# Six plain chunks instead of five at the start of three FFNs, and the normalised input formed in one piece on VectorE

## The chip, the core and the metric

The kernel runs on one core of a Trainium2 chip. The core has TensorE (PE in the rows; PEld is its weight load), VectorE (DVE), ScalarE (ACT), GpSimd (POOL) and SyncE (SP), which here only issues DMAs. The metric is the device time of one execution in microseconds; lower is better.

## What is computed

A small encoder on 528 tokens (16 meta tokens and 512 frames) of width 1024: two layers, each of an FFN, a token mixer and another FFN, with a residual add around each. There are thus four FFNs, and the change touches three of them. One FFN is

```python
def rmsnorm(x, g):
    xf = xf * lax.rsqrt(jnp.mean(xf * xf, axis=-1, keepdims=True) + EPS)
    return xf.astype(x.dtype) * g

def swiglu(h, w_gate, w_up, w_down):            # 1024 -> 2816 -> 1024
    return (jax.nn.silu(h @ w_gate) * (h @ w_up)) @ w_down

h = h + 0.5 * swiglu(rmsnorm(h, ffn1_norm[l]), ffn1_w_gate[l], ffn1_w_up[l], ffn1_w_down[l])
```

All data are float32.

## The kernel before

The residual `h` lies transposed: eight tiles of 128 channels by 528 tokens, one for each `c` of `KC = 8`. TensorE takes float32 products as three products of rounded halves: every operand is split into a high part (a ScalarE copy to `fp32r`) and a low part (a VectorE subtraction of the high part), and high·high, high·low and low·high are added in PSUM. For a weight tile of 128x1024 `fetch` does this: a DMA into `raw` (two buffers), the copy of L169, the subtraction of L170. For other tiles `split_to` does it (L183, L184). So each weight and each input costs VectorE an instruction of its own.

An FFN has 22 chunks `f` of 128 hidden channels. A *plain* chunk (`gate_up_plain`, L371) multiplies gate and up in the direct way: for gate and for up 8 pieces of K, 3 products of parts, 2 halves of the tokens, 96 matmuls in all. A *form* chunk (`gate_up`, L383) uses a Strassen-like scheme with 7 products in the place of 8: 7 x 4 x 3 = 84 matmuls. It needs sums of the weights (`bring_sums`, `bring`, `add_up`, `two_forms`, gathered in `prepare`) and sums of the input (`sums_x`, L245 to L248). `begun` is the number of the first form chunk: 5 in three FFNs, 2 in the third FFN of the program, whose input arrives normalised (`normed`).

The three FFNs without `normed` start with the 1/rms of their input unknown. `first_chunks` handles this. Chunks 0 and 1 run on the input without 1/rms, and their results are scaled later (chunk 0's are parked in `held`). Meanwhile 1/rms is found in two steps: `rms[0]` sums squares by matmul (L275), takes a power on GpSimd (L283) and puts the result on diagonals (L292, L294); `rms[1]` spreads it over all partitions by matmul (L303) and copies it out of PSUM (L307, L305). Then `normal_x` forms, for each of the eight `c`, the normalised input `xn` (L224) and splits it; chunk 2 runs by pieces of K (`by_chunk`), so that each piece can start when its `c` is split. From chunk 3 on the input is there.

The order on each engine is not the order of the source. When the program is built, a list scheduler places the instructions, with the source order as priority and its own estimate of when operands and buffers are there; what is ready earlier may go ahead. At run time each engine takes its queue in the placed order, and an instruction that waits holds up all that are behind it. Buffers come from pools: 48 slots for token tiles, 14 for split weights, 2 `raw`, 4 `half`, 4 `sum`, and 6 PSUM banks and one pair of banks.

The down products run one block of chunks later (`down_steps`, L193): eight parts `d` for each block, dealt out over three places in each form chunk. For block 1 (chunks 4 to 7) the number of places is three times the number of its form chunks: nine before.

Of the kernel before, what the change touches and what calls it, by code (L numbers as in the profile page):

```python
# [13 lines left out]
AF = mybir.ActivationFunctionType  # L14
ALU = mybir.AluOpType
# [10 lines left out]
KC = D // P  # L26
# [67 lines left out]
def trunk(ctx: ExitStack, tc, h0, wall, vecs, band, rope, out):  # L94
# [85 lines left out]

    def split_to(dst, src):

        nc.scalar.activation(dst[0], src, AF.Copy)  # L183
        nc.vector.tensor_tensor(dst[1], src, dst[0], op=ALU.subtract)  # L184

    def parts(T):
        return ((0, 264), (264, 528)) if T == L else ((0, T),)
# [30 lines left out]
    def normal_x(xs, c, g, t0, r):  # L218


        T = L - t0
        n = T // 2
        xn = xs["n"][c] = slot()[:, :T]
        nc.vector.scalar_tensor_tensor(xn, h[c][:, t0:L], gain(g + c), r, op0=ALU.mult, op1=ALU.mult)  # L224
        if c >= KC // 2:
            p = slot(F32R)[:, :T], slot(F32R)[:, :T]
            split_to(p, xn)
            xs["b"][c] = [(p[0][:, a : a + n], p[1][:, a : a + n]) for a in (0, n)]
            return
        xs["b"][c] = []  # L230
        for a in (0, n):
            t = slot(F32R)
            p = t[:, :n], t[:, n : 2 * n]
            split_to(p, xn[:, a : a + n])
            xs["b"][c].append(p)

    def sums_x(xs, k):


        xa, xb = xs["n"][k], xs["n"][k + KC // 2]  # L240
        T = xa.shape[-1]
        n = T // 2
        a1, a2, b1, b2 = (t[:, a : a + n] for t in (xa, xb) for a in (0, n))
        sub, stt = nc.vector.tensor_tensor, nc.vector.scalar_tensor_tensor
        sub(a1, a1, a2, op=ALU.subtract)  # L245
        sub(a2, b2, a2, op=ALU.subtract)
        stt(b2, b2, -1.0, a1, op0=ALU.mult, op1=ALU.subtract)
        stt(b1, b1, -1.0, b2, op0=ALU.mult, op1=ALU.subtract)  # L248
        out = []
        for t in (xa, xb):  # L250
            p = slot(F32R)[:, :T], slot(F32R)[:, :T]
            split_to(p, t)
            out += [(p[0][:, a : a + n], p[1][:, a : a + n]) for a in (0, n)]
        xs["t"][k] = [out[0], out[3], out[1], out[2]]
# [73 lines left out]
        return after  # L328


    def fetch_gate_up(u0, one=fetch):
        one(u0)
        one(u0 + 1)

    def ffn(u0, x, g, rms, t0, after, early=None, final=None, normed=None, hooks=()):

# [30 lines left out]
        def plain(w, o, xs, ks=range(KC)):  # L367
            for k in ks:
                for n, (a, b) in enumerate(((0, 0), (0, 1), (1, 0))):
                    for i, ps in enumerate(o):  # L370
                        nc.tensor.matmul(  # L371
                            ps,
                            w[a][:, k * P : k * P + P],
                            xs[k][i][b],
                            start=k == 0 and n == 0,
                            stop=k == KC - 1 and n == 2,
                        )
# [18 lines left out]
        def bring_sums(f):  # L396

            if f < NF:
                t = pair_of_sums()
                gate, up = wall[u0 + 3 * f], wall[u0 + 3 * f + 1]  # L400
                nc.sync.dma_start(t[:, 0], gate[:, :512])
                nc.sync.dma_start(t[:, 1], up[:, 512:])
                nc.gpsimd.dma_start(t, up[:, :512].unsqueeze(1).to_broadcast([P, 2, 512]), accum_op=ALU.add)  # L403
                forms[f] = {"s31": t}

        def bring(f):
            if f < NF:
                forms[f]["gate"] = load(u0 + 3 * f)
                t = forms[f]["up"] = half()
                nc.sync.dma_start(t, wall[u0 + 3 * f + 1][:, 512:])  # L410
# [39 lines left out]
        def evacuate(f, pg, pu, r=None):  # L450

            t, s = slot()[:, :T], slot()[:, :T]
            mult = nc.vector.tensor_tensor
            for ps, c0, c1 in pg:
                if r is None:
                    nc.scalar.activation(t[:, c0:c1], ps, AF.Silu)
                else:
                    mult(t[:, c0:c1], ps, r[:, c0:c1], op=ALU.mult)
            if r is not None:
                nc.scalar.activation(t, t, AF.Silu)  # L460
                mult(t, t, r, op=ALU.mult)
            for ps, c0, c1 in pu:
                mult(s[:, c0:c1], ps, t[:, c0:c1], op=ALU.mult)
            close(f, s)
# [8 lines left out]
        def gate_up_plain(f, by_chunk=False, pair=False):  # L473
            w_g, w_u = weights(f)
            pg = banks(2)
            pu = [ps for ps, _, _ in group_pair(T)] if T == L and (by_chunk or pair) else banks(2)
            if by_chunk:
                for k in range(KC):
                    plain(w_g, pg, x["b"], (k,))
                    plain(w_u, pu, x["b"], (k,))  # L480
                hook()
            else:
                plain(w_g, pg, x["b"])
                hook()
                plain(w_u, pu, x["b"])
            evacuate(f, by_halves(pg), by_halves(pu))
            hook()
# [42 lines left out]

        def first_chunks():

            nonlocal x
            w_g, w_u = weights(0)
            halves = [[(hi[:, a : a + N], lo[:, a : a + N]) for a in (0, N)] for hi, lo in x]
            pg, pu = banks(2), banks(2)
            for k in range(KC):
                for w, o in ((w_g, pg), (w_u, pu)):
                    plain(w, o, halves, (k,))
            held = []  # L540
            for o in (pg, pu):
                t = slot()[:, :T]
                for ps, c0, c1 in by_halves(o):
                    nc.scalar.activation(t[:, c0:c1], ps, AF.Copy)
                held.append([(t, 0, T)])
            fetch_gate_up(u0 + 3)
            rms[0]()
            w_g, w_u = weights(1)
            pg, pu = banks(2), banks(2)
            plain(w_g, pg, halves)  # L550
            r = rms[1]()
            fetch_gate_up(u0 + 6)
            xs = new_x()
            for c in range(KC):
                normal_x(xs, c, g, t0, r)
            plain(w_u, pu, halves)
            evacuate(1, by_halves(pg), by_halves(pu), r)
            x = xs
            fetch_gate_up(u0 + 9)
            sums_x(x, 0)  # L560
            gate_up_plain(2, True)
            fetch_gate_up(u0 + 12)
            sums_x(x, 1)
            sums_x(x, 2)
            gate_up_plain(3)
            bring_sums(5)
            bring(5)
            evacuate(0, *held, r)
            sums_x(x, 3)
            bring_sums(6)  # L570
            gate_up_plain(4, pair=True)
            prepare(5)
            bring(6)

        def first_chunk():
            nonlocal x
# [46 lines left out]

            return [lambda d=d: part(d) for d in range(KC)]

        begun = 5 if normed is None else 2
        for b, blk in enumerate(BLOCKS):

            n = 3 * sum(f >= begun for f in blk)
# [30 lines left out]
    x = []  # L660
# [622 lines left out]
```

## Time and profile before

| | |
|---|---|
| time, median of 3 runs | 1699.82 us (1695.87 to 1700.03) |
| profiled execution, its own time | 1702.0 us |
| its span, first to last instruction | 1700.2 us |
| PE, PEld busy | 1637.3, 1555.5 us |
| DVE, ACT, POOL busy | 1142.5, 809.5, 221.9 us |
| mean granted TensorE clock | 0.981 |

Busy times are sums over the whole span. A stretch with other limits than the rest does not show in them; it is seen in the slices, in the windows of a stretch, and in what each engine waited for. A row of the timeline gives the start of a merged group of instructions, its length, the engine, the line, the operation and the count, and in brackets the idle time in front of it with the instruction that ended it.

### The profile page before, as it was taken

What the parts mean: (1) busy time and instruction counts of PE and PEld (TensorE: products, weight loads), DVE (VectorE), ACT (ScalarE), POOL (GpSimd) and SP (SyncE); (2) the same over time, 40 slices, a digit from 0 to 9 for tenths busy, and PEclk for the clock granted to TensorE, in tenths of its full rate; (3) what the DMA queues carried; (4) which work ended last, traced back from release to release, by engine and by line L of the source; (5) the groups of instructions that cost most, each with busy time, mean ns of one, the idle gap of its engine ahead of it and who ended that gap; (6) DMA issues with size and microseconds to landing.
All of it is one profiled execution on the core that took longest, in us unless ns stands there. A gap on an engine that the chain in (4) does not pass through costs nothing.

```text
span 1700.2 us, 30059 instructions
## 1 busy us (share of the span) xinstructions
PE 1637.3 (96%) x11976; PEld 1555.5 (91%) x11976; DVE 1142.5 (67%) x1851; ACT 809.5 (48%) x1489; POOL 221.9 (13%) x257
## 2 busy tenths in 40 slices
PE   7999999998999999999899999999899899999997
PEld 7899999997999999999899999898787798999897
DVE  6865666657776566657767667566787766666655
ACT  6543444446454444445454444445576453444443
POOL 2000000005200000002000000001454100000002
PEclk9999999997999999999999999999899899999998
DMA  7455465533244555534355565643102434565411
GB/s 250 112 137 149 139 160 139 141 111 109 75 113 137 148 146 136 138 101 149 88 135 150 153 145 152 152 126 111 50 14 75 124 96 132 142 160 148 134 56 61
DMA packets 166206, 212.20 MB, mean 125 GB/s; under 512 B 10288, under 2 KB 102576, under 8 KB 166064
## 3 DMA queue, kind: packets, MB, share of 16 engines
q1 hardware_dynamic: 146176, 172.60, 32.2%
q0 software_dynamic: 19312, 37.23, 13.3%
q8 instruction: 94, 1.54, 0.4%
q10 hardware_dynamic: 576, 0.43, 0.1%
q14 instruction: 48, 0.39, 0.1%
HBM read 208.12 MB, written 2.10 MB: 124 GB/s over the span
## 4 chain that ended last, share of the span: by engine, by line
PE 84%; DVE 8%; DMA 3%; ACT 3%; issue 1%; POOL 0%; SPq 0%; DVEq 0%; ACTq 0%; POOLq 0%
PE ps L383 41%; PE ps L193 32%; PE ps L371 7%; DMA raw<-wall 2%; DVE t L184 2%; DVE t L224 1%; DVE w L170 1%; PE ps L1065 1%; DMA half<-wall 1%; ACT w L183 1%; DVE w L184 1%; PE ps L978 1%; PE ps L734 0%; PE ps L933 0%; ACT t L990 0%
## 5 line engine op out<-in xcount | busy, mean ns | idle before, releaser
L383 PE MATMUL ps<-t,w 128*128 128x256 f32 (+1 forms) x5964 | 757.1, 283 | 7.9 <-ACT t L525 6.7
L383 PEld LDWEIGHTS ps<-t,w 128*128 128x128 f32 x5964 | 740.1, 188 | 21.0 <-ACT t L525 8.1
L193 PE MATMUL ps<-t,w 128*128 128x264 f32 (+2 forms) x3672 | 628.4, 322 | 6.6 <-ACT t L183 2.0
L193 PEld LDWEIGHTS ps<-t,w 128*128 128x128 f32 x3672 | 527.9, 188 | 54.3 <-ACT t L183 5.0
L183 ACT ACTIVATE w<-half 128x512 fp32r<-128x512 f32 (+1 forms) x263 | 154.6, 603 | 230.8 <-PE ps L383 122.4
L371 PE MATMUL ps<-t,w 128*128 128x264 f32 (+1 forms) x1632 | 222.0, 297 | 21.5 <-DVE t L184 10.1
L371 PEld LDWEIGHTS ps<-t,w 128*128 128x128 f32 x1632 | 211.7, 199 | 30.1 <-DVE t L184 15.0
L403 POOL DMA_DIRECT2D sum<-wall x71 | 86.2, 1215 | 1077.9 <-DMA sum<-wall 400.6
L183 ACT ACTIVATE w<-sum 128x1024 fp32r<-128x1024 f32 x142 | 149.9, 1057 | 161.1 <-PE ps L383 108.2
L184 DVE TENSOR_TENSOR w<-half,w 128x512 fp32r<-128x512 f32 (+1 forms) x263 | 168.4, 655 | 70.6 <-ACT w L183 69.0
L184 DVE TENSOR_TENSOR w<-sum,w 128x1024 fp32r<-128x1024 f32 x142 | 173.1, 1220 | 54.3 <-PE ps L383 36.8
L614 DVE SCALAR_TENSOR_TENSOR h<-ps,h 128x528 f32<-128x528 f32 (+1 forms) x160 | 111.6, 697 | 140.1 <-PE ps L193 139.8
L183 ACT ACTIVATE t<-t 128x528 fp32r<-128x528 f32 (+4 forms) x174 | 99.0, 593 | 115.8 <-DVE t L526 62.9
L521 DVE TENSOR_TENSOR t<-ps,t 128x256 f32<-128x256 f32 (+1 forms) x71 | 30.3, 427 | 139.4 <-PE ps L383 138.5
L184 DVE TENSOR_TENSOR t<-t,t 128x528 fp32r<-128x528 f32 (+4 forms) x174 | 109.3, 643 | 11.2 <-ACT t L183 9.9
L184 DVE TENSOR_TENSOR w<-raw,w 128x1024 fp32r<-128x1024 f32 x71 | 86.7, 1221 | 28.1 <-PE ps L383 20.5
L183 ACT ACTIVATE w<-raw 128x1024 fp32r<-128x1024 f32 x71 | 74.9, 1055 | 55.5 <-PE ps L383 26.0
L170 DVE TENSOR_TENSOR w<-raw,w 128x1024 fp32r<-128x1024 f32 (+1 forms) x52 | 67.3, 1297 | 22.7 <-ACT w L169 21.1
L169 ACT ACTIVATE w<-raw 128x1024 fp32r<-128x1024 f32 (+1 forms) x55 | 54.5, 994 | 54.3 <-DMA raw<-wall 23.1
L263 POOL TENSOR_TENSOR t<-t,t 128x528 f32<-128x528 f32 (+1 forms) x33 | 52.9, 1603 | 156.4 <-ACT t L262 99.1
L513 ACT ACTIVATE t<-ps 128x256 f32<-128x256 f32 (+1 forms) x71 | 27.3, 385 | 81.8 <-PE ps L383 81.2
L211 DVE SCALAR_TENSOR_TENSOR t<-h,vt,t 128x528 fp32r<-128x528 f32 (+1 forms) x48 | 52.2, 1107 | 6.3 <-ACT t L210 6.1
(167 smaller groups left out, 1080.5 us busy)
## 6 DMA issues: line engine op xcount, KB each, us to landing
raw<-wall SPq DMA_DIRECT2D x118, 512.0 KB, 3.4
half<-wall SPq DMA_DIRECT2D x199, 256.0 KB, 3.8
sum<-wall SPq DMA_DIRECT2D x142, 256.0 KB, 3.2
sum<-wall POOLq DMA_DIRECT2D x71, 512.0 KB, 7.0
half<-wall SPq DMA_DIRECT2D x64, 192.0 KB, 2.8
h<-h SPq DMA_DIRECT2D x8, 264.0 KB, 5.6
raw<-wall SPq DMA_DIRECT2D x8, 256.0 KB, 4.0
raw<-band SPq DMA_DIRECT2D x4, 464.0 KB, 4.1
```

The costliest lines, as they stand in the source:

```text
L169: nc.scalar.activation(wh[:, a:b], raw[:, a:b], AF.Copy)
L170: low.tensor_tensor(wl[:, a:b], raw[:, a:b], wh[:, a:b], op=ALU.subtract)
L183: nc.scalar.activation(dst[0], src, AF.Copy)
L184: nc.vector.tensor_tensor(dst[1], src, dst[0], op=ALU.subtract)
L193: nc.tensor.matmul(ps, w[a], x[b][:, c0:c1], start=first and n == 0, stop=last and n == 2)
L211: nc.vector.scalar_tensor_tensor(xl, src, gain(g + c), xh, op0=ALU.mult, op1=ALU.subtract)
L263: (nc.vector if last else nc.gpsimd).tensor_tensor(ssq, ssq, sq, op=ALU.add)
L371: nc.tensor.matmul(ps, w[a][:, k * P : k * P + P], xs[k][i][b], start=k == 0 and n == 0, stop=k == KC - 1 and n == 2,)
L383: nc.tensor.matmul(ps, w[a][:, k * P : k * P + P], xs[k][b], start=first and k == 0 and n == 0, stop=last and k == 3 and n == 2, skip_grou ...
L403: nc.gpsimd.dma_start(t, up[:, :512].unsqueeze(1).to_broadcast([P, 2, 512]), accum_op=ALU.add)
L521: add(u[:, first], pd, u[:, first], op=ALU.add)
L614: nc.vector.scalar_tensor_tensor(hv, at, 0.5, hv, op0=ALU.mult, op1=ALU.add)
```

## The change

Three things in `first_chunks`, and two that follow from them:

- The rows of 1/rms are spread (`rms[1]`) after six of the eight pieces of K of chunk 1's gate, no longer after all eight.
- What is traced after the eight `normal_x` is put into a block that gives each VectorE instruction of the block an ordering edge to the last low part of the normalised input: it comes after that in VectorE's queue. The edge is for VectorE alone; ScalarE, SyncE, GpSimd and TensorE get none, and what is traced ahead of the block (the splits of chunk 2's weights, the evacuation of chunk 1) gets none either.
- Chunk 5 is plain in these three FFNs (`begun = 6`); the forms of 6 and 7 are brought in the place of those of 5 and 6. With two form chunks in block 1 its places for down parts are six.
- `evacuate(0, ...)`, the late scaling of chunk 0, stands after chunk 4 and no longer before it; the pair of PSUM banks is used by chunk 5 and no longer by chunk 4.
- `split_to` returns its two instructions; `fetch_gate_up` loses a parameter that was not used.

```diff
     def split_to(dst, src):
-        nc.scalar.activation(dst[0], src, AF.Copy)
-        nc.vector.tensor_tensor(dst[1], src, dst[0], op=ALU.subtract)
+        return (
+            nc.scalar.activation(dst[0], src, AF.Copy),
+            nc.vector.tensor_tensor(dst[1], src, dst[0], op=ALU.subtract),
+        )
...
-            split_to(p, xn)
+            _, xs["low"] = split_to(p, xn)
...
-            plain(w_g, pg, halves)
+            plain(w_g, pg, halves, range(6))
             r = rms[1]()
+            plain(w_g, pg, halves, range(6, KC))
             fetch_gate_up(u0 + 6)
             xs = new_x()
             for c in range(KC):
                 normal_x(xs, c, g, t0, r)
             plain(w_u, pu, halves)
             evacuate(1, by_halves(pg), by_halves(pu), r)
             x = xs
-            fetch_gate_up(u0 + 9)
-            sums_x(x, 0)
-            gate_up_plain(2, True)
-            fetch_gate_up(u0 + 12)
-            sums_x(x, 1)
-            sums_x(x, 2)
-            gate_up_plain(3)
-            bring_sums(5)
-            bring(5)
-            evacuate(0, *held, r)
-            sums_x(x, 3)
-            bring_sums(6)
-            gate_up_plain(4, pair=True)
-            prepare(5)
-            bring(6)
+            with tc.issue_after(xs["low"].ins):
+                fetch_gate_up(u0 + 9)
+                sums_x(x, 0)
+                gate_up_plain(2, True)
+                fetch_gate_up(u0 + 12)
+                sums_x(x, 1)
+                sums_x(x, 2)
+                gate_up_plain(3)
+                fetch_gate_up(u0 + 15)
+                sums_x(x, 3)
+                gate_up_plain(4)
+                evacuate(0, *held, r)
+                bring_sums(6)
+                bring(6)
+                bring_sums(7)
+                gate_up_plain(5, pair=True)
+                prepare(6)
+                bring(7)
...
-        begun = 5 if normed is None else 2
+        begun = 6 if normed is None else 2
```

## Rows read from the trace of the kernel before

**Rows 1.** The page: busy times, share of the span, instructions.
```profile
PE 1637.3 (96%) x11976; PEld 1555.5 (91%) x11976; DVE 1142.5 (67%) x1851; ACT 809.5 (48%) x1489; POOL 221.9 (13%) x257
```
**Rows 2.** Windows of the three openings: us; PE, PEld, DVE, ACT, POOL busy (count); PEclk; DMA share; GB/s.
```profile
31.16:82.79 51.63, 46.50 (x337) 44.45 (x337) 45.08 (x78) 26.91 (x47) 2.44 (x2) 0.93 0.44 123
448.92:491.35 42.43, 41.92 (x338) 41.23 (x338) 39.20 (x72) 20.73 (x39) 2.44 (x2) 1.00 0.36 88
1336.54:1389.47 52.93, 48.46 (x339) 45.28 (x338) 40.93 (x74) 22.98 (x43) 2.48 (x2) 0.87 0.34 89
37.76:54.40 16.64, 11.52 (x72) 9.68 (x72) 16.64 (x34) 7.00 (x12) 1.24 (x1) 0.95 0.57 154
54.40:60.00 5.60, 5.60 (x26) 5.60 (x27) 4.33 (x10) 3.19 (x4) 0.00 (x0) 0.52 0.32 110
1342.44:1355.70 13.26, 9.05 (x38) 6.66 (x38) 13.26 (x30) 5.62 (x12) 0.00 (x0) 0.78 0.53 120
1355.70:1364.00 8.30, 8.04 (x35) 7.46 (x36) 6.99 (x15) 5.30 (x8) 0.00 (x0) 0.52 0.00 0
```
**Rows 3.** Timeline of PE, first FFN: chunk 1, chunks 2 to 4, chunk 5, first down part.
```profile
23.89 6.13 PE L371 MATMUL ps<-t,w 128*128 128x264 f32 x48
31.16 6.60 PE L371 MATMUL ps<-t,w 128*128 128x264 f32 x52
...
51.73 31.23 PE L371 MATMUL ps<-t,w 128*128 128x264 f32 x224 [2.56 <-DVE t L184]
...
82.79 11.85 PE L383 MATMUL ps<-t,w 128*128 128x264 f32 x96
94.47 2.23 PE L193 MATMUL ps<-t,w 128*128 128x264 f32 x17
```
**Rows 4.** Timeline of PE, second FFN's chunks 2 to 4, fourth FFN's chunk 0.
```profile
466.91 24.60 PE L371 MATMUL ps<-t,w 128*128 128x264 f32 x200 [0.23 <-DVE t L184]
...
1316.65 11.49 PE L371 MATMUL ps<-t,w 128*128 128x256 f32 x96
```
**Rows 5.** Groups by line and shape, DVE from 33 to 57.5 us: count, busy us, mean ns, idle.
```profile
L224 DVE SCALAR_TENSOR_TENSOR t<-h,vt,t 128x528 f32<-128x528 f32 x8 | 6.1, 760 | 0.0
L170 DVE TENSOR_TENSOR w<-raw,w 128x1024 fp32r<-128x1024 f32 x4 | 4.9, 1221 | 2.6 <-ACT w L169 2.6
L184 DVE TENSOR_TENSOR t<-t,t 128x264 fp32r<-128x264 f32 x8 | 3.2, 426 | 0.0
L184 DVE TENSOR_TENSOR t<-t,t 128x528 fp32r<-128x528 f32 x4 | 2.8, 698 | 0.0
```
**Rows 6.** Timeline of the first FFN around 1/rms and the norms (first and last L224).
```profile
25.54 0.61 DVE L294 TENSOR_SCALAR t<-ident,s 128x128 f32<-128x128 f32 x3 [1.32 <-POOL s L283]
32.68 0.58 ACT L307 ACTIVATE t<-ps 128x512 f32<-128x512 f32 x1
33.95 0.76 DVE L224 SCALAR_TENSOR_TENSOR t<-h,vt,t 128x528 f32<-128x528 f32 x1
35.92 0.72 ACT L183 ACTIVATE t<-t 128x264 fp32r<-128x264 f32 x2
54.27 0.76 DVE L224 SCALAR_TENSOR_TENSOR t<-h,vt,t 128x528 f32<-128x528 f32 x1
```
**Rows 7.** Timeline of the fourth FFN around 1/rms.
```profile
1335.22 0.48 DVE L294 TENSOR_SCALAR t<-ident,s 128x128 f32<-128x128 f32 x2
1336.82 0.60 ACT L307 ACTIVATE t<-ps 128x512 f32<-128x512 f32 x1
1339.15 0.69 DVE L421 TENSOR_TENSOR sum<-sum,raw 128x512 f32<-128x512 f32 x1 [3.45 <-DMA raw<-wall]
1341.62 1.41 DVE L224 SCALAR_TENSOR_TENSOR t<-h,vt,t 128x512 f32<-128x512 f32 x2
```
**Rows 8.** Page, groups and DMA issues: down parts' residual; raw loads, us to landing.
```profile
L614 DVE SCALAR_TENSOR_TENSOR h<-ps,h 128x528 f32<-128x528 f32 (+1 forms) x160 | 111.6, 697 | 140.1 <-PE ps L193 139.8
raw<-wall SPq DMA_DIRECT2D x118, 512.0 KB, 3.4
```

More of the change, by code (lines that the diff above doesn't have):

```diff
@@ L328, in prep, with fetch_gate_up @@
         return after
-    def fetch_gate_up(u0, one=fetch):
-        one(u0)
-        one(u0 + 1)
+    def fetch_gate_up(u0):
+        fetch(u0)
+        fetch(u0 + 1)
     def ffn(u0, x, g, rms, t0, after, early=None, final=None, normed=None, hooks=()):
```

## The prediction

> **What bounds the kernel now.** I read the page's busy line first [rows 1]: TensorE is busy 96% of the span, so most stretches are bound by its matmuls. Then I cut out the stretch that the change rewrites: from the end of the spread of 1/rms to the first form product. It holds half of chunk 1 and chunks 2 to 4, 48 + 288 = 336 matmuls, in each of the three FFNs (the windows of [rows 2]).
>
> What those matmuls need when nothing holds them up is in the second FFN: 200 from 466.91 to the first form product at 491.35 us, 24.44/200 = 0.1222 us each; in the fourth, where a half is 256 tokens wide, 96 in 11.49 us, less some 0.15 by which the last one's row outlasts its issue, 0.118 us each [rows 2, 4]. So 336 need 41.06 us (39.65 in the fourth). They took 51.63, 42.43 and 52.93 us [rows 2]. Lost: 10.57 + 1.37 + 13.28 = 25.2 us.
>
> Where: in the first FFN VectorE is busy for all 16.64 us from 37.76 to 54.40, TensorE for 11.52 of them [rows 2]. TensorE waits for low parts (L184), 2.56 us at once ahead of 51.73 [rows 3]. The norms (L224) run from 33.95 to 54.27, 20 us for eight [rows 6], and chunk 2 can't run ahead of them. The work of the norms is 6.1 + 3.2 + 2.8 = 12.1 us [rows 5]; the rest of those 20 us is other work that the queue holds between them, as three splits of weights of L170 (1.22 us each, and idle time for their ScalarE copy) and sums of the input [rows 5]. After the waits the granted clock was 0.52 from 54.40 to 60, and again 0.52 from 1355.70 to 1364 [rows 2], the lower level of 1.2 GHz for nearly all of these stretches: part of the 25.2 us is the clock, and the second FFN, with waits under 1 us, shows 1.00 throughout.
>
> **What the change does, part by part.**
>
> *One more plain chunk:* 96 matmuls for 84, 12 x 0.1222 = 1.47 us in two FFNs and 12 x 0.118 = 1.42 in the fourth, 4.35 us in all, on TensorE's path. A form product costs the same per matmul (96 from 82.79 to 94.47, 0.1217 us, [rows 3]). VectorE loses the chunk's forms and gets two splits. DMA and GpSimd each have less to do; neither is late here, so I count nothing for them.
>
> *Spreading after six pieces of K:* the spread starts 12 x 0.1222 = 1.47 us earlier if the diagonals are there. In the first FFN TensorE would come to it at 23.89 + 36 x 0.1222 = 28.3 us [rows 3]; the diagonals were done by 26.2 [rows 6]. In the fourth the last diagonal was done at 1335.70 [rows 7], about when TensorE came; there TensorE may wait up to 1.4 us, but the same edge takes the later weight splits out of VectorE's queue ahead of the diagonals, so I take 0.3. The 12 matmuls left then run after the spread: no cost. On ScalarE the copy L307 came at 32.68 [rows 6], although TensorE had left the spread by 31.16 [rows 3]: other work stood ahead in that queue. It may stay there (norms start at 33.95 as now) or start when the spread ends (norms at about 31.1). I keep both.
>
> *The norms in one piece:* eight in at most 12.1 us [rows 5]. The first split piece is there 0.76 + 0.72 + 0.85 = 2.3 us after the start (L224, the two copies of L183, two of L184 [rows 5, 6]), at 33.4 to 36.3 us, before chunk 1 ends at 37.76 [rows 3]. After that the norms need 1.5 us for each `c` and TensorE 12 x 0.1222 = 1.47 for each piece, so TensorE follows without a wait, and the clock has no reason to fall. In the fourth FFN the norms waited for an `add_up` (L421, 3.45 us idle for a DMA) although 1/rms was copied by 1337.4 [rows 7]; the edge puts that behind them, and they start some 4 us earlier. The 25.2 us go, less what follows.
>
> *What now queues behind the norms:* the low parts of the weights of chunks 3, 4 and 5, the input sums, the evacuations, the forms of 6. The first of these that TensorE needs is chunk 3's gate, at 37.76 + 96 x 0.1222 = 49.5 us. The norms end at 43.2 to 46.1; the evacuation of chunk 1 may go ahead (four multiplications of halves at 0.43, two full ones at 0.7, about 3.1 us by the like shapes of [rows 5]) and then one split, 1.22 us: 47.5 to 50.4. So between 2 us in hand and 0.9 us late; I take 0.3 us for each FFN. A `raw` buffer comes free with each split and is filled again in 3.4 us [rows 8]; with ScalarE's and VectorE's part (2.5 us if ScalarE's copy takes as long as VectorE's 1.22 [rows 5]) chunk 4's weights are ready some 10 us before TensorE wants them (12 us later than chunk 3's). Behind SyncE's wait for that buffer stand only loads for chunk 6 and the down parts, wanted over 30 us later. The whole opening, now 444 matmuls or 54.3 us, must hold VectorE's 45.1 us [rows 2] plus two splits and a chunk's evacuation, about 4 us: it fits, with 5 us in hand.
>
> *Moved:* the scaling of chunk 0 after chunk 4 (four VectorE instructions of 0.7 us) is first read by a down part in chunk 6; its cover is chunk 5's 11.7 us, and without that it would cost 2.8. The bank pair used by chunk 5 instead of 4: chunk 4 takes banks that chunk 2's and 3's gate evacuations on ScalarE have freed a half chunk earlier; nothing. The returned tuple and the dropped parameter issue nothing.
>
> *Down parts on six places:* all eight parts of block 0 now fall in pairs into less than two form chunks. Two successive parts share one PSUM pair, and the second waits for the residual (0.70 us [rows 8]) unless form products lie between. 96 such matmuls are there for seven gaps of about 0.9 us, 7 matmuls each: enough. From zero to four uncovered gaps of 0.95 us in two FFNs (the fourth fits a pair of parts into one pair of banks): 0 to 7.6 us, and I take 1.
>
> *The sum:* -25.2 + 4.35 + 0.3 + 0.9 + 1 = -18.7 us. The profiled execution's own time, 1702.0 us, becomes 1683.3; it lies 2.2 us over the median of the runs, so against 1699.82 the forecast is **1681 us**.
>
> **A rule against it.** The Trainium skill, "Perfetto Trace Analysis", section "Identifying the Most-Contended Engine", has one take the engine of the highest occupancy as the one to relieve, and judge TensorE by its weight loads' busy share. That share is 91% here [rows 1], and the change adds 36 weight loads and matmuls to this engine: by the rule alone it loses. The same page, under "Optimization Strategy", says that the regimes of a kernel can differ, and that is what the windows show: the weight loads are at 9.68 of 16.64 us where VectorE is full [rows 2].
>
> **The rivals.**
>
> *TensorE is the bound in the openings too, or the edge doesn't keep the norms together:* other work (chunk 1's evacuation, late splits) still lies between the norms, and the waits stay. Then only the 4.35 us are added, less up to 1.47 for each FFN's earlier start: 1700 to 1704 us. Against it: the waits of TensorE name L184, and the three splits between the norms stand inside the block. The rule above, taken alone, gives this end.
>
> *The norms go in one piece but in series:* L224, its ScalarE copies and its low parts without overlap are 2.3 us for each `c`, 18.6 us in all. Chunk 2 ends 1.5 us late, chunk 3's gate is split at about 53.3, and each FFN loses 3.8 us: -25.2 + 4.35 + 11.4 = -9.5, or 1690 us. For it: ScalarE also has weight copies in its queue that wait for DMAs. Against it: with eight norms ready, the next L224 can fill each gap.
>
> *The same, and the clock falls (slower):* if that wait at chunk 3 lowers the clock in all three FFNs as after the waits of now (by the granted clocks, 0.05 x 16.64 + 0.48 x 5.6 = 3.5 us lost in the first FFN, 0.22 x 13.26 + 0.48 x 8.3 = 6.9 in the fourth [rows 2]), each loses 7.3 to 10.7 us: -25.2 + 4.35 + 22 to 32, 1701 to 1711 us. It decides from norms of 2.3 us each or more.
>
> *The down parts wait:* four uncovered gaps in two FFNs, 7.6 instead of 1: 1687.5 us.
>
> **How the numbers follow.** Forecast 0.70 (1677 to 1685: the norms' start and the queue behind them at either end, 0 to 3 us of new waits, and 2 us as the runs spread). Down parts 0.10, series 0.10, no gain 0.06, slower with the clock 0.04. The range is 1676 to 1690. 0.3%, which is 5.1 us, is about what a measurement of this kernel can tell from no change; faster by more has 0.90, within it 0.06, slower 0.04.
>
> **What would show it.** Right: L224 eight times within 13 us with only L184 between; no TensorE idle over 0.5 us in chunk 2; a granted clock of 1.00 from the spread to the first form product, 444 matmuls in some 54.5 us (52.5 in the fourth); the first FFN should gain about 8.5 us, the fourth about 11, and the second lose under 1, as it had only 1.4 us to give. Wrong: a wait of TensorE for L170 at chunk 3, a clock of 0.5 after it, or waits of L193 for L614 in chunks 6 and 7. The forecast fails most likely by the order that the scheduler gives to ScalarE's queue, which no row of before shows.

## The result, and the profile after

The changed kernel takes 1681.62 us (median of 4 runs, 1679.24 to 1682.65), the kernel before 1698.65 beside it: a ratio of 0.990, 95% interval 0.9882 to 0.9918. That is faster by more than the 0.3% that can be told from no change, and 0.6 us from the forecast. The profiled execution took 1680.98 us (span 1679.1, before 1700.2). In after.py most lines are two higher than in the kernel before: L373 for the plain chunks, L385 for the form chunks, L195 for the down parts, L226 for the norms, L185 for the low parts, L305 for the spread.

The busy line of the page after, to set beside [rows 1]:

```profile
PE 1624.8 (97%) x12012; PEld 1548.8 (92%) x12012; DVE 1131.7 (67%) x1833; ACT 802.8 (48%) x1471; POOL 220.8 (13%) x254
```

TensorE has 36 matmuls more, and yet less busy time: slow matmuls, which count as busy for longer, are gone together with the waits. "Perfetto Trace Analysis" of the Trainium skill (section "Identifying the Most-Contended Engine") judges TensorE's headroom by the share of its peak that its matmuls reach or by its weight loads' busy share, and says to optimize the most contended engine first. Read as the prediction read it, as work to be taken off TensorE, this is not borne out here: that share rose from 91% to 92% while the kernel became 1% faster.

The windows of the three openings after, from the end of the spread to the first form product; they hold a plain chunk more than those of [rows 2]. Columns as there.

```profile
30.29:84.37 54.08, 54.08 (x445) 54.08 (x445) 47.89 (x82) 30.49 (x52) 2.44 (x2) 1.00 0.49 146
439.05:493.11 54.06, 54.06 (x446) 54.06 (x446) 46.74 (x81) 27.62 (x49) 2.44 (x2) 1.00 0.46 132
1325.11:1379.79 54.68, 53.65 (x447) 52.83 (x446) 46.45 (x81) 29.47 (x51) 2.48 (x2) 1.00 0.46 136
```

In the first two TensorE is busy all the time at a granted clock of 1.00: 444 x 0.1222 = 54.26 us is what the matmuls need, and nothing is lost. In the fourth FFN 444 x 0.118 = 52.4 us are needed and 54.68 taken, 2.3 us lost. The timeline of TensorE over the first and the fourth opening (start, length, engine, line, count, and in brackets the idle time ahead):

```profile
28.99 1.37 PE L305 MATMUL ps<-t,ones 128*128 128x128 f32 x10
30.29 54.25 PE L373 MATMUL ps<-t,w 128*128 128x264 f32 x444
84.37 5.75 PE L385 MATMUL ps<-t,w 128*128 128x264 f32 x46
...
1325.11 12.68 PE L373 MATMUL ps<-t,w 128*128 128x256 f32 x102
1338.37 0.50 PE L373 MATMUL ps<-t,w 128*128 128x256 f32 x2 [0.58 <-ACT t L184]
1339.10 6.40 PE L373 MATMUL ps<-t,w 128*128 128x256 f32 x52 [0.22 <-DVE t L185]
1345.65 34.30 PE L373 MATMUL ps<-t,w 128*128 128x256 f32 x288 [0.16 <-DVE t L465]
```

The first FFN's 444 matmuls are one group without a gap, where [rows 3] has a wait of 2.56 us. The fourth still waits for the last of the norms. VectorE's queue over the end of the norms in the first FFN, to set beside [rows 6], shows why:

```profile
34.36 0.76 DVE L226 SCALAR_TENSOR_TENSOR t<-h,vt,t 128x528 f32<-128x528 f32 x1
35.04 0.78 DVE L185 TENSOR_TENSOR t<-t,t 128x264 fp32r<-128x264 f32 x2
35.73 0.77 DVE L226 SCALAR_TENSOR_TENSOR t<-h,vt,t 128x528 f32<-128x528 f32 x1
...
40.67 0.71 DVE L185 TENSOR_TENSOR t<-t,t 128x528 fp32r<-128x528 f32 x1 [0.71 <-ACT t L184]
41.30 0.76 DVE L226 SCALAR_TENSOR_TENSOR t<-h,vt,t 128x528 f32<-128x528 f32 x1
42.77 0.71 DVE L185 TENSOR_TENSOR t<-t,t 128x528 fp32r<-128x528 f32 x1 [0.71 <-ACT t L184]
43.40 0.76 DVE L226 SCALAR_TENSOR_TENSOR t<-h,vt,t 128x528 f32<-128x528 f32 x1
44.93 0.71 DVE L185 TENSOR_TENSOR t<-t,t 128x528 fp32r<-128x528 f32 x1 [0.77 <-ACT t L184]
45.56 0.77 DVE L460 TENSOR_TENSOR t<-ps,t 128x264 f32<-128x264 f32 x2
46.24 1.22 DVE L170 TENSOR_TENSOR w<-raw,w 128x1024 fp32r<-128x1024 f32 x1
```

The eight norms stand in one piece, from 31.81 to 45.64 us, with nothing but L185 between them. The first two stand back to back, and the third, fourth and fifth start 1.37 us apart. From the fifth on the tiles are split whole, and the norms start 2.1 us apart: the low parts of the last three each wait 0.7 us for ScalarE's copy of their own norm, and the next norm stands behind the low part. Chunk 3's gate is split at 46.24 to 47.46; TensorE comes to it at 30.29 + 156 x 0.1222 = 49.4 us.

The next table shows where the 21.1 us between the two spans come from. It goes by the starts of chunk 0 and of the first form product of each FFN in TensorE's timeline. An opening runs from chunk 0 to the end of chunk 5; the first one is counted from the span's start. Where chunk 5 is a form chunk, its 84 matmuls are added at 10.22 us (9.95 in the fourth FFN), so waits in it fall into the rest.

| us | first | second | fourth | rest of the span |
|---|---|---|---|---|
| before | 93.0 | 72.6 | 82.8 | 1451.9 |
| after | 84.4 | 72.6 | 72.0 | 1450.1 |

The first opening gains 8.6 us, the second nothing, the fourth 10.7, and 1.8 us lie in the rest.

### The profile page after: what moved, and what is told of

It is laid out like the page before. It is cut to its first block, busy times and chain, and to the rows that moved or that the text cites. A ratio compares the mean times of both kernels' runs of the same rounds, so it can differ in the third digit from the quotient of the medians.

```text
span 1679.1 us, 30041 instructions
## 1 busy us (share of the span) xinstructions
PE 1624.8 (97%) x12012; PEld 1548.8 (92%) x12012; DVE 1131.7 (67%) x1833; ACT 802.8 (48%) x1471; POOL 220.8 (13%) x254
## 4 chain that ended last, share of the span: by engine, by line
PE 87%; DVE 6%; ACT 3%; DMA 2%; issue 1%; POOL 0%; SPq 0%; DVEq 0%; ACTq 0%; POOLq 0%
PE ps L385 40%; PE ps L195 32%; PE ps L373 11%; DMA half<-wall 1%; DVE t L185 1%; PE ps L1072 1%; DVE w L170 1%; ACT w L184 1%; DVE t L226 1%; PE ps L985 1%; DVE t L213 1%; PE ps L741 0%; ACT t L184 0%; ACT t L997 0%; DVE w L185 0%
## 5 line engine op out<-in xcount | busy, mean ns | idle before, releaser
L385 PE MATMUL ps<-t,w 128*128 128x256 f32 (+1 forms) x5712 | 725.2, 283 | 8.8 <-ACT t L527 6.7
L385 PEld LDWEIGHTS ps<-t,w 128*128 128x128 f32 x5712 | 708.5, 188 | 22.0 <-ACT t L527 8.1
L195 PE MATMUL ps<-t,w 128*128 128x264 f32 (+2 forms) x3672 | 626.5, 321 | 6.4 <-ACT t L184 2.0
L195 PEld LDWEIGHTS ps<-t,w 128*128 128x128 f32 x3672 | 527.2, 188 | 54.3 <-ACT t L184 5.0
L373 PE MATMUL ps<-t,w 128*128 128x264 f32 (+1 forms) x1920 | 242.8, 288 | 12.9 <-ACT w L169 5.3
L373 PEld LDWEIGHTS ps<-t,w 128*128 128x128 f32 x1920 | 237.7, 192 | 16.2 <-ACT t L184 5.4
L405 POOL DMA_DIRECT2D sum<-wall x68 | 82.6, 1215 | 1062.7 <-DMA sum<-wall 443.1
L184 ACT ACTIVATE w<-sum 128x1024 fp32r<-128x1024 f32 x136 | 143.4, 1058 | 154.2 <-PE ps L385 116.6
L185 DVE TENSOR_TENSOR w<-half,w 128x512 fp32r<-128x512 f32 (+1 forms) x260 | 166.6, 655 | 73.2 <-ACT w L184 71.9
L185 DVE TENSOR_TENSOR w<-sum,w 128x1024 fp32r<-128x1024 f32 x136 | 165.6, 1220 | 28.8 <-PE ps L385 16.3
L185 DVE TENSOR_TENSOR t<-t,t 128x528 fp32r<-128x528 f32 (+4 forms) x174 | 109.3, 646 | 19.3 <-ACT t L184 17.7
L185 DVE TENSOR_TENSOR w<-raw,w 128x1024 fp32r<-128x1024 f32 x68 | 83.1, 1222 | 29.8 <-PE ps L385 21.4
L169 ACT ACTIVATE w<-raw 128x1024 fp32r<-128x1024 f32 (+1 forms) x61 | 60.8, 1001 | 59.2 <-DMA raw<-wall 37.0
L170 DVE TENSOR_TENSOR w<-raw,w 128x1024 fp32r<-128x1024 f32 (+1 forms) x58 | 74.7, 1296 | 8.9 <-ACT w L169 8.0
```

The lines of the kernel that those rows point to most:

```text
L169: nc.scalar.activation(wh[:, a:b], raw[:, a:b], AF.Copy)
L170: low.tensor_tensor(wl[:, a:b], raw[:, a:b], wh[:, a:b], op=ALU.subtract)
L184: nc.scalar.activation(dst[0], src, AF.Copy),
L195: nc.tensor.matmul(ps, w[a], x[b][:, c0:c1], start=first and n == 0, stop=last and n == 2)
L373: nc.tensor.matmul(ps, w[a][:, k * P : k * P + P], xs[k][i][b], start=k == 0 and n == 0, stop=k == KC - 1 and n == 2,)
L385: nc.tensor.matmul(ps, w[a][:, k * P : k * P + P], xs[k][b], start=first and k == 0 and n == 0, stop=last and k == 3 and n == 2, skip_grou ...
```

## The experiments

Each ran beside the kernel before on the same chip; the openings of all of them stand in one table behind the last. Edits are shown against the kernel after.

**The edge taken away.** Theory A: the ordering edge, which keeps the norms in one piece, is the whole gain; theory B: the sixth chunk as cover is.

```diff
-            with tc.issue_after(xs["low"].ins):
-                fetch_gate_up(u0 + 9)
+            fetch_gate_up(u0 + 9)
...
```

The rest of the block stands outside in the same way.

> The changed kernel without the ordering edge: six plain chunks and the early spread of 1/rms stay, the block is traced as plain source. Theory A (the norms kept together are the gain): the splits, sums and add_ups come back between the eight norms, TensorE waits for L185 in chunk 2 of the first and fourth FFN for some 9 and 11 us as before, the clock falls there, and the 4.35 us of the sixth chunk are paid on top: 1697 to 1704 us, ratio to the kernel before 0.999 to 1.003. Theory B (the sixth chunk gives VectorE the time, the edge only shapes the order): the waits shrink anyway, 1680 to 1688 us. Theory C (the early start of 1/rms is the gain): 1683 to 1690 us.

Measured: 1702.7 us, ratio 1.0016 (1.0003 to 1.0029). All of the gain is gone. The norms take 32.26 to 55.78 us, with splits of weights and sums of the input between them, and TensorE waits in chunk 2 of the first FFN:

```profile
31.77 13.91 PE L373 MATMUL ps<-t,w 128*128 128x264 f32 x112
45.97 2.12 PE L373 MATMUL ps<-t,w 128*128 128x264 f32 x12 [0.29 <-DVE t L185]
49.09 2.11 PE L373 MATMUL ps<-t,w 128*128 128x264 f32 x12 [1.01 <-DVE t L185]
53.25 39.02 PE L373 MATMUL ps<-t,w 128*128 128x264 f32 x308 [2.05 <-DVE t L185]
```

Without the edge the sixth chunk and the earlier spread bring nothing.

**Five plain chunks again, with the edge.** The scaling of chunk 0 stands where it stood before, ahead of chunk 4.

```diff
-                fetch_gate_up(u0 + 15)
-                sums_x(x, 3)
-                gate_up_plain(4)
+                bring_sums(5)
+                bring(5)
                 evacuate(0, *held, r)
+                sums_x(x, 3)
                 bring_sums(6)
-                bring(6)
-                bring_sums(7)
-                gate_up_plain(5, pair=True)
-                prepare(6)
-                bring(7)
+                gate_up_plain(4, pair=True)
+                prepare(5)
+                bring(6)
...
-        begun = 6 if normed is None else 2
+        begun = 5 if normed is None else 2
```

> Edge and early spread stay, chunk 5 is a form chunk again (forms of 5 and 6 brought where they were, nine places for the first down parts). Theory A (the sixth plain chunk is only a cost of 4.35 us, paid for nothing): 1677 to 1678 us, ratio 0.987. Theory B (it is cover: what the edge pushed behind the norms, 35.55 us of VectorE in the 38.73 us from 45.64 to the first form product in the first FFN, would need to be done in 27 us): the first form product waits some 4 to 6 us in each FFN, with or without a lower clock, against 1.45 us saved: 1687 to 1695 us, ratio 0.993 to 0.998, and TensorE's longest wait of the opening stands at L385 or in chunk 4, not in chunk 2.

Measured: 1693.03 us, ratio 0.9964 (0.9952 to 0.9976), 11 us worse than after although TensorE has 36 matmuls less. Chunks 2 to 4 run without a gap, and then, inside form chunk 5 (L385) and ahead of a down part of the fourth FFN (L195):

```profile
73.35 5.64 PE L385 MATMUL ps<-t,w 128*128 128x264 f32 x45
81.64 0.59 PE L385 MATMUL ps<-t,w 128*128 128x264 f32 x1 [2.65 <-ACT t L184]
82.47 5.65 PE L385 MATMUL ps<-t,w 128*128 128x264 f32 x24 [0.24 <-DVE t L185]
...
1384.20 0.50 PE L195 MATMUL ps<-t,w 128*128 128x512 f32 x1 [3.31 <-ACT t L184]
```

This is theory B. Of the two theories of the first experiment neither holds alone: the edge gives the gain, and the sixth chunk keeps it, since what the edge pushes behind the norms has to go somewhere. The 24 form matmuls in 5.65 us at 82.47 are 0.235 us each, nearly twice 0.1217: a slow stretch follows the wait, with a granted clock of 0.50.

**The spread after all eight pieces of K.**

```diff
-            plain(w_g, pg, halves, range(6))
+            plain(w_g, pg, halves)
             r = rms[1]()
-            plain(w_g, pg, halves, range(6, KC))
```

> The spread of 1/rms goes back behind all eight pieces of K of chunk 1's gate; the rest is the changed kernel. Theory A (the norms have some 4 us in hand ahead of chunk 2 and lose 1.47 us of it): the first and second FFN stay as they are; in the fourth, where TensorE already waits 0.6 us for the last norms, up to 1.4 us are added: 1681.5 to 1684 us. Theory B (the start of the norms is on the path): 1.4 us in each FFN, 1686 us.

Measured: 1686.71 us, ratio 0.9926 (0.9913 to 0.9938). The time is that of theory B, the stages are not. The openings of the first and second FFN stay, as in theory A; the fourth is 2.4 us longer, 1.0 more than theory A allowed. There short waits in chunk 2 are followed by a granted clock of 0.50 from 1343.70 to 1347.12 us; at half speed these 3.4 us cost some 1.7 of the 2.4 (an estimate). The other 3.7 us of the span lie in stretches that this edit does not touch (more on that below).

**The norms in series.** Each norm gets an edge to the low part of the one before it.

```diff
-            split_to(p, xn[:, a : a + n])
+            _, xs["low"] = split_to(p, xn[:, a : a + n])
...
-            for c in range(KC):
-                normal_x(xs, c, g, t0, r)
+            normal_x(xs, 0, g, t0, r)
+            for c in range(1, KC):
+                with tc.issue_after(xs["low"].ins):
+                    normal_x(xs, c, g, t0, r)
```

> The eight norms in series: an edge puts each L226 behind the last low part of the norm ahead of it, the rest is the changed kernel. The last four run so already (2.1 us apart), so the piece grows from 13.8 to some 17 us. Rival of the prediction with the clock kept: chunk 2 ends 1 to 2 us late and chunk 3's bank or gate another 1, 2.5 to 3.8 us for each FFN, 1689 to 1693 us. Rival with the clock falling: 7 to 10 us for each FFN, 1703 to 1713 us, granted clock 0.5 for some us after the waits. If the cover is longer than I count, under 2 us in all.

Measured: 1689.54 us, ratio 0.9943 (0.9931 to 0.9955). By its total this is the rival "in series, the clock kept" (1690); by its stages it is not. The norms of the first FFN take 16.6 us. From the end of the spread on, its opening is only 0.1 us longer (54.19 us for 54.08); the 1.2 us more ahead of that are chunk 1's clock (last section). The second opening gains and loses nothing, and the fourth is 3.7 us longer, where the rival had 3.8 in each. Nor was the clock kept. Its mean over the span stays at 0.988, but in the fourth FFN, behind short waits in chunk 2 (0.2 to 0.6 us each), it fell:

```profile
1346.35:1349.77 3.42, 3.37 (x15) 3.07 (x16) 3.42 (x8) 2.65 (x3) 0.00 (x0) 0.50 0.05 6
```

At half speed this stretch costs some 1.7 of the 3.7 us (an estimate). The rest of the difference is again in untouched stretches.

**The kernel after once more, unaltered**, beside the two following ones:

> The changed kernel once more, unaltered, beside the two experiments that follow, on the chip that they run on. It measures how far one build repeats: if the differences of some 2 us that e3_late_spread and e4_series showed in stretches that they do not touch come from the build (the order that the list scheduler gives to distant instructions), this run repeats the stages of the changed kernel within 0.3 us (openings 60.5, 72.6 and 72.0 us, first form product of the second FFN to chunk 0 of the third 319.5) and its ratio of 0.990 within 0.001. If they come from one execution to the next, its stages differ by as much as theirs.

Measured: 1683.43 us against 1700.28, ratio 0.9903 (0.9887 to 0.9919). The second and fourth opening repeat within 0.03 us. The rest of the span repeats within 0.1 us as a sum; the four stretches that it consists of differ by up to 0.5. In e1, e3 and e4 the rest is 3 to 4 us longer. Two differences show in the traces. Up to chunk 0 of the third FFN VectorE and ScalarE take their instructions in another order after each of these edits, and there e3 is 2.2 and e4 2.7 us longer. From the first form product of the third FFN on, the order of operations on every engine is the same in all of these kernels, and still e1 takes 4.8 us more up to chunk 0 of the fourth FFN (the kernel after, then e1):

```profile
844.90:1307.75 462.85, 446.96 (x2868) 401.29 (x2867) 316.32 (x554) 239.19 (x470) 92.29 (x129) 0.99 0.42 116
```
```profile
854.47:1322.13 467.66, 451.25 (x2867) 404.86 (x2867) 316.21 (x554) 239.27 (x470) 91.65 (x129) 0.98 0.43 115
```

The clock was at 0.50 for 17.1 us of this stretch in e1 and for 6.8 in the kernel after. How much of such differences belongs to a build and how much to a single execution, one repeat does not tell. An edit is to be read from its own stage. Of the openings only the first differs, by 1.6 us, and that is chunk 1's clock (last section).

**The low part of each norm behind the next norm.**

```diff
-            for c in range(KC):
-                normal_x(xs, c, g, t0, r)
+            scaled_x(xs, 0, g, t0, r)
+            for c in range(KC - 1):
+                ahead = scaled_x(xs, c + 1, g, t0, r)
+                with tc.issue_after(ahead.ins):
+                    parts_x(xs, c, t0)
+            parts_x(xs, KC - 1, t0)
```

`scaled_x` is the norm's multiplication (L226) alone, `parts_x` its copies and low parts.

> The norms are written out so that the low part of one piece stands behind the multiplication of the next one, so that VectorE has work while ScalarE copies. In the changed kernel the last four norms run in series, 2.1 us apart, with VectorE idle 0.7 us in each, and the piece takes 13.8 us. Theory (the series is the only thing left that holds the openings): the piece shrinks to 11 or 12 us, the openings of the first and second FFN stay (they have cover), the fourth gains what TensorE still waits there, 1 to 2 us: 1679.5 to 1681 us in all. Rival (ScalarE's copies set the pace, and the order on VectorE is indifferent): the piece stays at 13 us or more, and the fourth opening stays at 72.0 us or gets longer.

Measured: 1679.44 us, ratio 0.9876 (0.986 to 0.9893), the fastest kernel here; the interval just overlaps that of the unaltered kernel (0.9887 to 0.9919). The norms take 32.14 to 43.14 us, 11.0 for 13.8. From the end of the spread on the first opening does not move (54.10 us for 54.08), nor does the second; the fourth is 2.2 us shorter, and its matmuls run without a gap (lines are 6 higher here):

```profile
1326.43 52.75 PE L379 MATMUL ps<-t,w 128*128 128x256 f32 x444
```

That is the 2.3 us which the fourth opening still lost.

**The edge on the weight splits alone**, and **on all but the weight splits**: what is it that tore the norms apart?

The first keeps it on the three `fetch_gate_up`:

```diff
+            low = xs["low"].ins
+            with tc.issue_after(low):
                 fetch_gate_up(u0 + 9)
-                sums_x(x, 0)
-                gate_up_plain(2, True)
+            sums_x(x, 0)
+            gate_up_plain(2, True)
...
```

and the second on every other step of the block:

```diff
+            low = xs["low"].ins
+            fetch_gate_up(u0 + 9)
+            with tc.issue_after(low):
                 sums_x(x, 0)
...
```

> The edge is kept on the low parts of the weights of chunks 3, 4 and 5 alone; the sums of the input, the evacuations and the forms of 6 and 7 have none. Theory (three weight splits are what tore the norms apart, as the prediction has it): the norms stay in one piece of 14 to 16 us, the openings lengthen by 0 to 2 us each, 1681 to 1685 us. Rival (the sums of the input and other work do as much as the splits): norms of 17 us or more, waits of TensorE for low parts in chunk 2, 1687 to 1695 us.

> The opposite: the edge is kept on all that stands in the block but the low parts of the weights of chunks 3, 4 and 5, which may go between the norms again. Theory (the weight splits tear them apart): the norms take 17 to 20 us, TensorE waits for low parts in chunk 2 of the first and the fourth FFN, with a clock near 0.5 behind it, and the time is 1692 to 1702 us. Rival (the splits alone do little; it takes the sums and the evacuations too): norms under 16 us and 1681 to 1687 us.

Measured: 1686.35 us, ratio 0.992 (0.9906 to 0.9933), for the first, a little over what was expected, and 1695.97, ratio 0.9981 (0.997 to 0.9991), for the second. With the edge on the splits alone the norms take 15.6 us in the first FFN, the fourth opening is 3.1 us longer, and the others 0.1 beyond a later end of the spread in the first. With the splits free the norms take 19.5, 15.7 and 14.0 us in the three FFNs (13.8, 13.4 and 13.0 in the kernel after), and the openings are 5.7, 1.8 and 6.0 us longer; 1.2 of the 5.7 lie ahead of the end of the spread. As means of its first and fourth opening the granted clock is 1.00 and 0.97. In the fourth it is 0.50 behind the last wait of chunk 2, as expected; in the first it stays at 1.00, also behind a wait of 2.17 us at 60.74:

```profile
1353.35:1356.77 3.42, 3.42 (x17) 3.42 (x18) 3.42 (x10) 2.86 (x3) 0.00 (x0) 0.50 0.93 147
```

So the six weight splits do most of the harm, as the prediction has it for its three; what else stands in the block, the sums of the input among it, does a part, mainly in the fourth FFN, which has no slack. Some 1.7 us of the 3.1 and of the 6.0 are the clock (a stretch of 3.4 us at 0.50 in each, an estimate). Half of the 6.0 us has another place, VectorE's queue ahead of the diagonals (L296) in the fourth FFN with the splits free:

```profile
1331.68 1.23 DVE L170 TENSOR_TENSOR w<-raw,w 128x1024 fp32r<-128x1024 f32 x1 [1.20 <-ACT w L169]
1332.82 0.15 DVE L284 TENSOR_SCALAR s<-ps 128x4 f32<-128x4 f32 x1
1334.92 1.23 DVE L170 TENSOR_TENSOR w<-raw,w 128x1024 fp32r<-128x1024 f32 x1 [1.94 <-ACT w L169]
1336.06 0.48 DVE L296 TENSOR_SCALAR t<-ident,s 128x128 f32<-128x128 f32 x2
```

and in the kernel after:

```profile
1320.10 0.16 DVE L284 TENSOR_SCALAR s<-ps 128x4 f32<-128x4 f32 x1 [2.16 <-PE ps L277]
1321.42 0.49 DVE L296 TENSOR_SCALAR t<-ident,s 128x128 f32<-128x128 f32 x2 [1.15 <-POOL s L285]
```

Splits of later chunks that wait for ScalarE stand ahead of the diagonals, and the norms begin later: the spread ends 20.5 us after the start of chunk 0, instead of 17.4. The edge takes them away from there too, although it names only the last low part.

**Five chunks with the overlapped norms.** Does the sixth chunk cover only the slow piece?

> Five plain chunks (as e2_five_chunks) with the norms written out as in e5_overlap: the piece of norms is 11 us, and chunk 5 is a form chunk again. It asks what the sixth chunk covers. Theory A (it covers only the slowness of the piece, 13.8 us and 0.7 us of idle VectorE in the last four norms): with a shorter piece the forms of chunk 5 come 2.5 us earlier, the waits of 2.65 to 3.3 us that e2_five_chunks had in form chunk 5 go, the openings are 1.5 us shorter than those of e5_overlap, and the time is 1675 to 1679 us. Theory B (it covers the whole of VectorE's work in the opening, which five chunks cannot hold): waits for L184 or L185 remain in form chunk 5 or in the down parts behind it, 1 to 3 us in each opening, part of a clock of 0.5 behind them, and the time is 1682 to 1692 us.

The edit is that of e2_five_chunks and that of e5_overlap together. Measured: 1686.48 us, ratio 0.9935 (0.9921 to 0.9948): theory B's time. The plain chunks run without a gap again; the wait in form chunk 5 is 1.31 us for 2.65, and the one ahead of the fourth FFN's down part is unchanged at 3.31:

```profile
1369.39 2.99 PE L391 MATMUL ps<-t,w 128*128 128x256 f32 x24
1375.70 4.68 PE L195 MATMUL ps<-t,w 128*128 128x512 f32 x12 [3.31 <-ACT t L184]
```

The last multiplication of chunk 0's late scaling (L471 on a tile, 128x512) runs just ahead of that, and ScalarE's copy, for which TensorE waits, waits for it:

```profile
1374.23 0.69 DVE L471 TENSOR_TENSOR t<-t,t 128x512 f32<-128x512 f32 x1
...
1375.01 1.67 ACT L184 ACTIVATE t<-t 128x512 fp32r<-128x512 f32 x3 [1.50 <-DVE t L471]
```

That is the moved step whose cover the prediction named.

**The same, with chunk 0's scaling ahead of chunk 2.**

```diff
                 sums_x(x, 0)
+                evacuate(0, *held, r)
                 gate_up_plain(2, True)
 ...
                 bring(5)
-                evacuate(0, *held, r)
                 sums_x(x, 3)
```

> As e8_five_overlap (five plain chunks, norms written out), and the late scaling of chunk 0 stands ahead of chunk 2 instead of behind chunk 3. In e8_five_overlap TensorE waits 1.31 us in form chunk 5 for a token tile split on ScalarE and 3.31 us in the fourth FFN ahead of the first down part, at the time at which the last instruction of that scaling (L471) and three splits of 128x528 tiles behind it run. Theory A (those waits are for the scaling of chunk 0, which the sixth chunk only covers by its 11.7 us): they go, and the openings end 4 to 5 us earlier than in e8_five_overlap, with 1677 to 1682 us in all. Theory B (VectorE's and ScalarE's work as a whole doesn't fit into five chunks): the same wait turns up at another tile (weights of chunk 5, L184 on w, or sums of the input), and the time stays at 1684 to 1690 us.

Measured: 1692.48 us, ratio 0.995 (0.9938 to 0.9962). Form chunk 5 now runs without a wait (96 matmuls from 77.55 in 11.82 us), so the waits there were for that scaling and what stood behind it. But they turn up elsewhere, and longer:

```profile
64.25 13.47 PE L379 MATMUL ps<-t,w 128*128 128x264 f32 x96 [3.35 <-ACT t L464]
...
1363.00 0.80 PE L195 MATMUL ps<-t,w 128*128 128x512 f32 x1 [7.51 <-ACT w L184]
```

The time is above theory B's range too (1684 to 1690), but the mechanism is theory B's as far as these orders go. Whether some other order fits five chunks was not tried.

The openings of all kernels, as in the table above:

| us | first | second | fourth | rest |
|---|---|---|---|---|
| before | 93.0 | 72.6 | 82.8 | 1451.9 |
| after | 84.4 | 72.6 | 72.0 | 1450.1 |
| after_again | 85.9 | 72.6 | 72.0 | 1450.1 |
| e1_no_edge | 92.1 | 75.9 | 82.2 | 1453.7 |
| e2_five_chunks | 83.6 | 71.2 | 70.6 | 1467.5 |
| e3_late_spread | 84.1 | 72.7 | 74.4 | 1453.8 |
| e4_series | 85.7 | 72.6 | 75.7 | 1452.9 |
| e5_overlap | 85.8 | 72.6 | 69.9 | 1449.6 |
| e6_free_splits | 90.1 | 74.4 | 78.0 | 1451.5 |
| e7_free_rest | 85.7 | 72.7 | 75.1 | 1449.3 |
| e8_five_overlap | 83.9 | 71.3 | 68.3 | 1460.4 |
| e9_early_scaling | 87.8 | 73.7 | 78.8 | 1452.0 |

In eight of the twelve executions (after_again, e1, e2 and e4 to e8) chunk 1 of the first FFN runs in part at the lower clock, which makes the first opening some 1.5 us longer, whatever the edit (last section). In e2_five_chunks and e8_five_overlap the openings look short, and the bill stands in the rest, 17 and 10 us over that of after: the waits and slow matmuls in form chunk 5 and behind it are in it.

## Why the prediction was right, step by step

*The bound, and the lost 25.2 us.* Right. The waits for low parts went with the norms in one piece, and the kernel without the edge has them back. Two of the three openings now lose nothing, the fourth 2.3 us. So of the signs that the prediction named, a clock of 1.00 and no wait over 0.5 us in chunk 2, the first two FFNs show both; the fourth has a wait of 0.58 us and needs 54.68 us for the 52.5 forecast.

*By FFN.* Predicted about 8.5, under 1 lost and about 11; measured 8.6, 0.0 and 10.7. The 8.6 compare two executions without the slow stretch in chunk 1; against after_again it would be 7.1. In the fourth the terms are -13.28 + 1.42 for the sixth chunk + 2.3 still lost - 1.1 for the earlier spread = -10.7. The last is 2.5 us by which the spread ends earlier after the start of chunk 0 (17.4 for 19.9) less the 1.42 of matmuls that only moved behind it.

*The sixth chunk.* Its price is right: the second opening had 1.37 us to lose and 1.47 to pay, and did not move. What the prediction said too little of is its worth. "It fits, with 5 us in hand" was reckoned for six chunks; that five do not fit in the orders tried is shown only by the runs. With five, e2 is 11 us slower than the kernel after, and e8 and e9 are 10 and 13 us slower than e5, which has the same norms (each by its ratio to the kernel before).

*The norms.* This step failed in part. "Eight in at most 12.1 us" and "the next L224 can fill each gap" hold for the first four norms alone; the piece takes 13.8 us because the last four run in series. The prediction had that as a rival for all eight, at 3.8 us for each FFN. Measured, it costs 0, 0 and 2.2 us, as the overlapped norms show: the first two FFNs have the slack. The queue's order, which no row of before shows, decided, but on VectorE; the last line of the prediction expected it on ScalarE.

*What queues behind the norms.* 0.9 us were taken. In the first two FFNs it is nothing: chunk 3's gate has 2 us in hand in the first, as at the better end of the estimate, and 3.4 in the second; in the fourth 0.16 us, for a bank that L465 frees late.

*The early spread.* The norms start at 31.81, between the two ends given (31.1 and 33.95). TensorE does not wait for the diagonals in the fourth FFN (0.3 taken), since VectorE has done its part by 1321.91 and ScalarE its own by 1322.11, well before the spread at 1324.30. From the end of the spread to the first norm it took 5.1 us there and takes 0.9, so the 4 us that the edge was to give are right. When it alone is undone (e3), the early spread is worth 2.4 us in the fourth FFN, some 1.7 of them through the clock, and nothing in the others.

*The late scaling of chunk 0.* "Without that it would cost 2.8": with five chunks the wait for it is 3.31 us in the fourth FFN.

*The down parts.* 1 us was taken, from up to eight gaps of 0.95 us, a figure that no row shows. In chunks 6 and 7 of the two FFNs TensorE waits once for the residual in the kernel after, 0.46 us at 514.19, and twice in after_again, 0.65 and 0.66. So the term is about right.

*The slower rival.* Behind the spread no opening of the kernel after shows the lower clock. With the norms in series one of three does, the fourth, behind waits in chunk 2 and not in chunk 3: the mechanism is there, but it costs some 1.7 us in one opening, where the rival had 3.5 to 6.9 us for the clock in each. Slow matmuls follow single waits of 1 to 3 us (without the edge 0.50 from 52.80 to 56.21 us, in chunk 2 of the first FFN; with five chunks 0.50 in form chunk 5) and rows of waits of 0.2 to 0.6 us, but not every wait: e6 keeps 1.00 behind 2.17 us.

*The sum.* From the profiled execution -18.7 us was forecast, and -21.0 measured (1702.0 to 1680.98); the openings give 19.3 of it. The prediction had a loss of 1 us for the rest, the down parts, and there 1.8 us were gained. A wait of a down part for the residual is gone (0.62 us at 1425.50) and another has come (0.46 at 514.19); the other 1.6 us are not assigned, and lie within what the untouched stretches differ by among the kernels above. By the medians it is 17.0 us, because the profiled execution of before lies 3.3 us over its median in that comparison and the one of after 0.6 under its own. The forecast took its 18.7 us off 1699.82, while the median beside the result is 1698.65. With the terms off by 1.7 to 2.3 us, an end within 0.6 us of the forecast is in part luck.

## What to carry to other kernels

When one engine serves both a chain that the bound engine waits for and work that is wanted later, look at what stands between the links of that chain in its queue, and hold the later work back with an edge; then ask where that work goes, and give it cover, even at the price of more work on the bound engine. After an edit under a list scheduler compare stages, not totals: here stages that the edit does not touch moved by up to 4.8 us, through another order or another clock. Look at the clock of a short stretch behind a wait, not at its mean over a stage: 3.4 us at 0.50 show as 0.97 over an opening.

## What the runs showed that was not expected

The clock of chunk 1 in the first FFN is one of two. The windows of 24 to 28 us of the kernel after, in its two profiled executions, first the one above and then after_again:

```profile
24.00:28.00 4.00, 4.00 (x34) 3.96 (x35) 1.00 (x7) 1.65 (x3) 1.20 (x1) 1.00 0.97 243
```
```profile
24.00:28.00 4.00, 4.00 (x26) 3.96 (x26) 0.96 (x7) 1.64 (x3) 1.20 (x1) 0.69 0.95 241
```

It is the same program with the same instructions: a granted clock of 1.00 with 34 matmuls, or of 0.69 (1.2 GHz for part of the time) with 26, and the first form product 1.6 us later. The record does not say whether both ran on the same chip. Ahead of it TensorE had been idle 1.47 us in the one and 2.23 in the other, with the 10 matmuls of the sums of squares between. But e7_free_rest has only 1.20 us of idle time there and the slow matmuls too (36 in 6.08 us), while the kernel before has 1.90 us and no slow matmuls (48 in 6.13 us). So the length of that wait alone does not decide it, and what does is open. The Trainium skill, "TensorE: Matmul & The Clock Gate", section "What's actually happening", says of the slow matmuls at the start of a kernel that their number differs between runs of one kernel. These two executions show such a difference 24 us into the kernel, behind a wait of 1.5 and 2.2 us.
